# A hybrid decoder layer on one core: token blocks taken one at a time, one block's MLP interleaved with the next block's attention

## The chip, the core and the metric

The kernel runs on one core of a Trainium2 chip. Its time is the device time of one execution in microseconds (us), the median of several runs. TensorE (PE) multiplies matrices into PSUM banks; VectorE (DVE), ScalarE (ACT) and GpSimd (POOL) work element by element; SyncE (SP) issues the DMA transfers. Each engine executes its own queue of instructions strictly in order and waits there for semaphores of the others, so the order in which the program is written decides what can run beside what.

## What is computed

One decoder layer over a prompt of 2,048 tokens and 64 sample tokens (8 sequences of 8), width 1,024. All weights are shared by both groups; there is one layer (DEPTH 1), then a final RMSNorm.

```python
def _mixer_in(x, g_mix, w_in):
    h = _rmsnorm(x, g_mix)
    proj = h @ w_in
    q = proj[..., :ATTN_WIDTH].reshape(B, L, N_KV_HEADS, GROUP, HEAD_DIM)
    ...
    u = proj[..., ATTN_WIDTH + 2 * KV_WIDTH:]
    return q, k, v, u
...
def _layer_tail(x, attn_o, pool_o, mem_k, mem_v, w_out, g_cross, w_cq, w_co, g_ffn, w_up, w_down):
    B, L, _ = x.shape
    x = x + jnp.concatenate([attn_o, pool_o], axis=-1) @ w_out
    h = _rmsnorm(x, g_cross)
    q = (h @ w_cq).reshape(B, L, N_CROSS_HEADS, CROSS_HEAD_DIM)
    s = jnp.einsum('blhd,bmhd->bhlm', q, mem_k).astype(jnp.float32) * (CROSS_HEAD_DIM ** -0.5)
    p = jax.nn.softmax(s, axis=-1)
    o = jnp.einsum('bhlm,bmhd->blhd', p.astype(mem_v.dtype), mem_v).reshape(B, L, D_MODEL)
    x = x + o @ w_co
    h = _rmsnorm(x, g_ffn)
    x = x + jnp.square(jax.nn.relu(h @ w_up)) @ w_down
    return x
...
    for l in range(DEPTH):
        q, k, v, u = _mixer_in(xp, g_mix[l], w_in[l])
        attn_o = _window_attn_prompt(q, k, v, attn_sinks[l])
        ...
        pool_o, pool_new = _pool_mix(u, u_prev, 0, w_pool[l], pool_scale[l])
        mem_k, mem_v = _mem_kv(mem_prompt, g_mem[l], w_ck[l], w_cv[l])
        xp = _layer_tail(xp, attn_o, pool_o, mem_k, mem_v, w_out[l], g_cross[l], w_cq[l], w_co[l],
                         g_ffn[l], w_up[l], w_down[l])
        ...
        q, k, v, u = _mixer_in(xs, g_mix[l], w_in[l])
        attn_o, k_buf, v_buf = _window_attn_sample(q, k, v, cache_win_k[l], cache_win_v[l], attn_sinks[l])
        ...
        xs = _layer_tail(xs, attn_o, pool_o, cache_mem_k[l], cache_mem_v[l], w_out[l], g_cross[l],
                         w_cq[l], w_co[l], g_ffn[l], w_up[l], w_down[l])
```

The attention has a window of 128 tokens, sinks and ALiBi; the pooling mixer subtracts causal means over 2, 4, 8 and 16 tokens. Keys and values of the memory (and the last window's keys, values and pool inputs) are outputs as well. All in fp32.

## The kernel before

**Products.** Every fp32 operand is split in two parts, hi and lo, of a rounded type, and each product is three matmuls: hi·hi, hi·lo, lo·hi (lines 111 to 113 in `mm3`, 280 to 282 in `dense`). Activations are kept with the width on the 128 partitions and tokens in the free dimension, so that a matmul has a 128x128 piece of a weight and as many columns as the block has tokens.

**Weights.** `Stream` holds the list of all weight tiles, 128x1024 each (512 KB), in order of use. `emit` takes one: SyncE loads it to a raw tile `f` (L131), ACT casts it to the hi tile (L132), DVE subtracts to the lo tile (L133); both are named `w` in the views. `next` hands out the oldest, `pump` prepares more while tiles are free. There are 12 `w` tiles (six pairs) and six raw tiles.

**Prologue.** `prologue` computes the memory's keys and values (weights `wck`, `wcv`), folds wcq into the keys (`a_s`, 8 tiles) and wco into the values (`b_s`, 8 tiles), so that cross attention of the prompt needs one product A to the scores and one product B back. The pool projection is folded into w_out (`wo_s`).

**Superblocks.** The tokens are six blocks: 384, 384, 384, 384, 256 and 256 + 64 sample. `SBLOCKS` puts them in three pairs. `superblock` takes a pair through all stages, and each weight pair that is handed out serves both blocks before it is given back (`order` and `seq` in `dense` set which block goes first in which chunk). Stages of a superblock: in-projection (10 weights); window attention (units of one 128-token tile and one of two key heads: QK L668, scores to a tile L669, normalise L690, transposes L699, product with v L716/L717); output projection (8 weights); cross attention (A 8 weights, softmax L929 to L935, transposes L911; B 8 weights); MLP with `up` and `down` alternating in groups of four weights (32 and 32). `mix` alternates attention's steps with the rest of the in-projection; the last superblock also mixes `cross` with `sample_cross`, which loads the samples' own memory (`wcq`, `cmk`, `cmv`, `wco`).

**Norms.** `Norm` squares on ACT (L205), adds on POOL (L206), sums over partitions by a matmul with ones (L214), takes ln and exp (L217 on), and `apply` scales and splits (L232 to L235). A list `later` with `flush` places a norm's second half behind some steps of the other block. The next superblock's first norm is emitted ahead of the last `down` groups.

**MLP.** After `up` a group is evacuated by ACT with relu (L1122), squared on POOL (L1123), cast on ACT (L1125), its lo part formed on DVE (L1126). `down` adds to x on DVE (L1156). A final norm (L1173) and the store of y (L1175) follow.

**PSUM.** Four `mm` banks for products, four `aux` banks for attention, norms and transposes.

Of the kernel before, what the change touches and what calls it, by code (L numbers as in the profile page):

```python
# [36 lines left out]
class Slots:  # L37
# [3 lines left out]

    def get(self):
        return self.free.popleft()
# [8 lines left out]
def kernel(ctx: ExitStack, tc: tile.TileContext, io, nW=12, nF=6, nT=8):  # L52
# [40 lines left out]

    def rnd(ps, hi, lo, scale=None):
        if scale is None:
            nc.scalar.copy(hi, ps)
            nc.vector.tensor_tensor(lo, ps, f32(hi), ALU.subtract)
# [10 lines left out]
    def mm3(ps, ks, Wh, Wl, Hh, Hl, first=True, final=True):  # L108
        last = len(ks) - 1
        for i, k in enumerate(ks):  # L110
            nc.tensor.matmul(ps, Wh(k), Hh(k), start=first and i == 0, stop=False)  # L111
            nc.tensor.matmul(ps, Wh(k), Hl(k), start=False, stop=False)  # L112
            nc.tensor.matmul(ps, Wl(k), Hh(k), start=False, stop=final and i == last)  # L113

    class Stream:
        def __init__(self):
# [3 lines left out]
            self.resF = 0  # L120

        def add(self, key, *raw, eng=None):
            self.items.append((key, raw, eng or nc.vector))

        def emit(self):
            key, raw, eng = self.items.popleft()
            th, tl = WS.get(), WS.get()
            r = FS.get()
# [4 lines left out]
            eng.tensor_tensor(tl[:], r[:, 0:1024], f32(th[:]), ALU.subtract)  # L133
            FS.put(r)
            self.ready.append((key, th, tl))

        def pump(self):
            while self.items and len(WS.free) - 2 >= self.resW and len(self.ready) < 5:
                if len(FS.free) - 1 < self.resF:
                    break  # L140
                self.emit()
# [9 lines left out]
    S = Stream()  # L151
    CIN = (0, 1, 2, 3, 4, 5, 6, 8, 7, 9)
    FINC, N1W, N1Q = 2, 4, 4
    N1C = ("ck", 4)
    LW = (0, 6, 6)
    for n in ("ck", "cv"):
        for c in range(8):
            S.add((n, c), io["w" + n][c])
    for c in range(8):
        S.add(("cq", c), io["wcqt"][c])  # L160
    for c in range(8):
        S.add(("co", c), io["wco"][c])
    for s in range(3):
        for c in CIN:
            S.add(("in", s, c), io["win"][c])
            if s == 0 and c in (0, 1):
                for g in range(2):
                    S.add(("wop", 2 * c + g), io["wop"][2 * c + g])
        for c in range(8):
            S.add(("wo", s, c), io["woa"][c], wo_s[c])  # L170
        for hf in range(2):
            for kp in range(4):
                S.add(("A", s, hf, kp), a_s[hf, kp])
        for c in range(8):
            S.add(("B", s, c), b_s[c])
        for g in range(9):
            for c in range(4):
                if g < 8:
                    S.add(("up", s, g, c), io["wup"][4 * g + c])
            for c in range(4):  # L180
                if g > 0:
                    S.add(("dn", s, g - 1, c), io["wdn"][4 * (g - 1) + c])

    class Norm:
# [5 lines left out]
        def sq(self, k, eng=None):  # L190
            n = self.n
            if self.on_pe:
                t = TS.get()
                if eng is None:
                    nc.scalar.activation(t[:, 0:n], self.x(k), AF.Square)
                else:
                    eng.tensor_tensor(t[:, 0:n], self.x(k), self.x(k), ALU.mult)
                nc.tensor.matmul(self.pm[:, 0:n], ones[:], t[:, 0:n], start=k == 0, stop=k == 7)
# [4 lines left out]
            else:  # L203
                t = TS.get()
                nc.scalar.activation(t[:, 0:n], self.x(k), AF.Square)  # L205
                nc.gpsimd.tensor_tensor(self.acc[:, 0:n], self.acc[:, 0:n], t[:, 0:n], ALU.add)  # L206
                TS.put(t)

        def fin(self):
            n = self.n  # L210
            pm = self.pm
            if not self.on_pe:
                pm = AUX.get()
                nc.tensor.matmul(pm[:, 0:n], ones[:], self.acc[:, 0:n], start=True, stop=True)  # L214
# [11 lines left out]
        def apply(self, g, hi, lo, piece=8):  # L226
            n = self.n
            for k in range(8):
                if k and k % piece == 0:
                    yield  # L230
# [27 lines left out]
    def order(nch, head, tail):  # L258
        out = []
        for lo_, hi_, outer in ((0, head, True), (head, nch - tail, False), (nch - tail, nch, True)):  # L260
            if outer:
                out += [(c, b) for b in (0, 1) for c in range(lo_, hi_)]
            else:
                out += [(c, b) for c in range(lo_, hi_) for b in (0, 1)]
        return out

    def dense(keys, blks, hi, lo, evac, head=2, tail=3, after=None, piece=8, seq=None):
        nch = len(keys)
        loaded, left, done = {}, {}, {0: 0, 1: 0}
        fetched = 0  # L270
        for c, b in seq or order(nch, head, tail):
            while fetched <= c:
# [1057 lines left out]
```

## Time and profile before

| | us |
|---|---|
| median of 3 runs | 2643.78 (2640.39 to 2644.97) |
| span of the profiled execution, first to last instruction | 2639.7 |
| ACT hi casts, 330 | 346.9 |
| DVE lo subtractions, 330 | 422.8 |
| relu, square and split of the MLP on POOL (L1123), 192 | 219.0 |
| additions of `down` on DVE (L1156), 384 | 199.7 |

The profile lists for each engine its busy time, for groups of instructions their number, busy time, mean duration and the idle time before them with the releaser, and for any stretch of time the busy time of each engine in it. `mm<-act,w` means that a tile named mm was written from tiles act and w. The number behind L is the line in the kernel. Matmuls overlap, so their durations (some 0.3 us) are longer than the distance from one start to the next; a stage's rate is better read as a number of matmuls in a stretch. By stretches, the prologue with the first norms takes 0 to about 132 us, then each superblock has a mixed part of some 396 us (in-projection, attention, projection, cross) and an MLP of 330 to 462 us.

### The profile page before, as it was taken

To read this page: it belongs to the slowest core of one execution; us is meant where nothing else is said; L and a number is where in the kernel's file an instruction comes from. 1 tells how busy PE (TensorE), PEld (TensorE's weight loads), DVE (VectorE), ACT (ScalarE), POOL (GpSimd) and SP (SyncE) were. 2 spreads that over 40 slices of the span, in tenths; PEclk is the share of its full clock that TensorE was granted. 3 is DMA by queue.
4 is the path that set the end of the run, shared out by engine and by line. 5 is a ranking of instruction groups with operands and counts; after the bars stand their busy time and mean duration, and the time that the engine had idled before them with its cause. 6 is when DMAs were issued, how large, how long until landed. Compare 5 with 4: busy or idle time off the path is not lost. (4 is left out here: it accounts for less than half of the span.)

```text
span 2639.7 us, 39195 instructions
## 1 busy us (share of the span) xinstructions
PE 2565.7 (97%) x15725; PEld 2458.0 (93%) x15725; DVE 1302.4 (49%) x2276; ACT 984.2 (37%) x1923; POOL 680.7 (26%) x730
## 2 busy tenths in 40 slices
PE   7899999999999999999999999999999999999998
PEld 7798979999999999997999999999999669999998
DVE  7568453633333357936363333334766646334334
ACT  6666342422222244834342222223355434332231
POOL 3215322411111153433241111113334214111111
PEclk9999999999999999999999999999999999999999
DMA  7843212211111123131111111112414473222210
GB/s 261 260 130 101 72 49 74 71 64 63 61 62 64 56 72 113 45 132 56 65 58 63 65 64 64 65 56 71 140 60 149 176 266 112 87 80 81 88 57 37
DMA packets 92251, 244.76 MB, mean 93 GB/s; under 512 B 16740, under 2 KB 31524, under 8 KB 90916
## 3 DMA queue, kind: packets, MB, share of 16 engines
q1 hardware_dynamic: 92068, 242.25, 26.9%
q8 instruction: 123, 2.02, 0.3%
q14 instruction: 60, 0.49, 0.1%
HBM read 219.53 MB, written 22.69 MB: 92 GB/s over the span
## 5 line engine op out<-in xcount | busy, mean ns | idle before, releaser
L281 PE MATMUL mm<-act,w 128*128 128x384 f32 (+2 forms) x2784 | 899.1, 323 | 6.5 <-DVE act L235 5.0
L280 PE MATMUL mm<-act,w 128*128 128x384 f32 (+2 forms) x2784 | 902.8, 324 | 2.5 <-ACT act L623 1.6
L282 PE MATMUL mm<-act,w 128*128 128x384 f32 (+2 forms) x2784 | 897.4, 322 | 1.1 <-DVE w L133 0.9
L132 ACT CAST w<-f 128x1024 fp32r<-128x1024 f32 x330 | 346.9, 1052 | 737.4 <-PE mm L112 453.9
L133 DVE TENSOR_TENSOR w<-f,w 128x1024 fp32r<-128x1024 f32 x330 | 422.8, 1286 | 317.9 <-ACT w L132 312.0
L111 PE MATMUL mm<-act,w 128*128 128x384 f32 (+2 forms) x1728 | 554.1, 321 | 13.6 <-ACT act L372 8.3
L112 PE MATMUL mm<-act,w 128*128 128x384 f32 (+2 forms) x1728 | 550.3, 318 | 0.0
L113 PE MATMUL mm<-act,w 128*128 128x384 f32 (+2 forms) x1728 | 549.8, 318 | 0.0
L281 PEld LDWEIGHTS mm<-act,w 128*128 128x128 f32 x2784 | 527.3, 189 | 16.3 <-DVE act L235 6.7
L280 PEld LDWEIGHTS mm<-act,w 128*128 128x128 f32 x2784 | 527.4, 189 | 7.2 <-issue 2.3
L282 PEld LDWEIGHTS mm<-act,w 128*128 128x128 f32 x2784 | 527.3, 189 | 1.8 <-DVE w L133 1.6
L1123 POOL TENSOR_TENSOR t<-t 128x384 f32<-128x384 f32 (+2 forms) x192 | 219.0, 1141 | 1034.8 <-ACT t L1122 1034.8
L1156 DVE TENSOR_TENSOR x<-mm,x 128x384 f32<-128x384 f32 (+2 forms) x384 | 199.7, 523 | 326.5 <-PE mm L113 326.5
L111 PEld LDWEIGHTS mm<-act,w 128*128 128x128 f32 x1728 | 328.6, 190 | 15.8 <-ACT act L372 8.3
L112 PEld LDWEIGHTS mm<-act,w 128*128 128x128 f32 x1728 | 328.3, 190 | 1.2 <-DVE act L373 0.2
L113 PEld LDWEIGHTS mm<-act,w 128*128 128x128 f32 x1728 | 328.4, 190 | 0.1
L206 POOL TENSOR_TENSOR t<-t,t 128x384 f32<-128x384 f32 (+2 forms) x168 | 203.0, 1209 | 348.9 <-ACT t L205 331.4
L1126 DVE TENSOR_TENSOR act<-t,act 128x384 fp32r<-128x384 f32 (+2 forms) x192 | 103.2, 537 | 300.4 <-ACT act L1125 300.4
L1125 ACT CAST act<-t 128x384 fp32r<-128x384 f32 (+2 forms) x192 | 93.8, 488 | 237.5 <-POOL t L1123 237.5
L1122 ACT ACTIVATE t<-mm 128x384 f32<-128x384 f32 (+2 forms) x192 | 88.2, 459 | 95.2 <-PE mm L282 94.2
L205 ACT ACTIVATE t<-x 128x384 f32<-128x384 f32 (+2 forms) x140 | 68.4, 499 | 145.4 <-DVE x L1085 64.9
L111 PE MATMUL mm<-w,act 128*128 128x512 f32 x288 | 116.7, 406 | 3.2 <-ACT f L330 1.7
(184 smaller groups left out, 2199.0 us busy)
## 6 DMA issues: line engine op xcount, KB each, us to landing
f<-in_wup SPq DMA_DIRECT2D x96, 512.0 KB, 3.5
f<-in_wdn SPq DMA_DIRECT2D x96, 512.0 KB, 3.5
f<-in_win SPq DMA_DIRECT2D x30, 512.0 KB, 3.6
f<-a_s SPq DMA_DIRECT2D x24, 512.0 KB, 3.2
f<-b_s SPq DMA_DIRECT2D x24, 512.0 KB, 4.2
x<-in_x SPq DMA_DIRECT2D x6, 1536.0 KB, 7.1
f<-in_wco SPq DMA_DIRECT2D x16, 512.0 KB, 4.9
f<-in_cmk SPq DMA_DIRECT2D x16, 512.0 KB, 4.5
```

The source lines that it names most:

```text
L111: nc.tensor.matmul(ps, Wh(k), Hh(k), start=first and i == 0, stop=False)
L112: nc.tensor.matmul(ps, Wh(k), Hl(k), start=False, stop=False)
L113: nc.tensor.matmul(ps, Wl(k), Hh(k), start=False, stop=final and i == last)
L132: nc.scalar.copy(th[:], r[:, 0:1024])
L133: eng.tensor_tensor(tl[:], r[:, 0:1024], f32(th[:]), ALU.subtract)
L206: nc.gpsimd.tensor_tensor(self.acc[:, 0:n], self.acc[:, 0:n], t[:, 0:n], ALU.add)
L280: nc.tensor.matmul(ps[:, 0:n], w8(th)[:, k, :], hi(b, k), start=k == 0, stop=False)
L281: nc.tensor.matmul(ps[:, 0:n], w8(th)[:, k, :], lo(b, k), start=False, stop=False)
L282: nc.tensor.matmul(ps[:, 0:n], w8(tl)[:, k, :], hi(b, k), start=False, stop=k == 7)
L1123: nc.gpsimd.tensor_tensor(q[:, 0:n], r[:, 0:n], r[:, 0:n], ALU.mult)
L1126: nc.vector.tensor_tensor(lo, q[:, 0:n], f32(hi), ALU.subtract)
L1156: nc.vector.tensor_tensor(bl.x(m), ps[:, 0:n], bl.x(m), ALU.add)
```

## The change

Blocks are no longer paired. `SBLOCKS` becomes six blocks, each through all stages on its own, and each weight is split anew for each block. Stages are generators: `early` (first norm, in-projection, pool mix, window attention, second load of x), `late_` (output projection, cross norm, the sample's cross attention in the last block, A, B, ffn norm), `mlp`, and `prologue`. They yield between small pieces of work, with a number: how many ns should pass, by an estimate of TensorE's time that `mmul` and `trans` keep in `busy`, before this generator is resumed. `run` interleaves several of them: it resumes the one that is least far along, as a share of the total given with it. At the end of the program these calls stand:

- the prologue with `early` of block 0;
- `late_` of block 0 with `early` of block 1;
- the MLP of block 0 with `late_` of block 1;
- the MLP of block s with `early` and `late_` of block s+1, for s = 1 to 4;
- the MLP of block 5 alone.

There are two weight streams. S1 has the in-, output, A and B weights of blocks 1 to 5 and block 0's in-projection, with six tiles `w0_` (three pairs, of which one holds the keys while attention runs) and four raw tiles `f`, shared with attention, folds and the sample's loads. S2 has the prologue, the rest of block 0 and all MLPs, with six tiles `w1_` and two raw tiles `g`. A and B weights are loaded straight to the lo tile, without a raw one (`ext=False`). PSUM: three `mm` banks for each stream and two `aux`. The prologue's order is now keys, A fold, values, B fold, pool fold, and the memory norm's squares are added on DVE. The cross attention loops over weights outside and tiles inside (`kp` before `c0`), its softmax following for the whole half. The samples' window outputs are copied DRAM to DRAM. The last block's final norm sums its squares on PE.

```diff
-SBLOCKS = [
-    [(0, 384, 0), (384, 384, 0)],
-    [(768, 384, 0), (1152, 384, 0)],
-    [(1536, 256, 0), (1792, 256, 64)],
-]
+SBLOCKS = [[(0, 384, 0)], [(384, 384, 0)], [(768, 384, 0)], [(1152, 384, 0)], [(1536, 256, 0)], [(1792, 256, 64)]]
+NBLK = 6
...
-    ACTS = Slots([sb(f"act{i}", 4 * NB, F32R) for i in range(16)])
-    WS = Slots([sb(f"w{i}", 1024, F32R) for i in range(nW)])
-    FS = Slots([sb(f"f{i}", 1088) for i in range(nF)])
-    TS = Slots([sb(f"t{i}", 400) for i in range(nT)])
-    XT = [sb(f"x{i}", 3136) for i in range(2)]
-    MM = Slots([psp.tile([P, 512], F32, name=f"mm{i}", tag=f"mm{i}") for i in range(4)])
-    AUX = Slots([psp.tile([P, 512], F32, name=f"aux{i}", tag=f"aux{i}") for i in range(4)])
+    ACTT = [sb(f"act{i}", 4 * NB, F32R) for i in range(16)]
+    ACTS = Slots(ACTT)
+    WS = [Slots([sb(f"w{q}_{i}", 1024, F32R) for i in range(6)]) for q in range(2)]
+    FS = [Slots([sb(f"f{i}", 1088) for i in range(4)]), Slots([sb(f"g{i}", 1024) for i in range(2)])]
+    F0 = FS[0]
+    TS = Slots([sb(f"t{i}", 400) for i in range(6)])
+    TM = Slots([sb(f"tm{i}", 384) for i in range(3)])
+    XT = [sb(f"x{i}", 3072) for i in range(2)]
+    MM = [Slots([psp.tile([P, 512], F32, name=f"mm{q}{i}", tag=f"mm{q}{i}") for i in range(3)]) for q in range(2)]
+    AUX = Slots([psp.tile([P, 512], F32, name=f"aux{i}", tag=f"aux{i}") for i in range(2)])
...
+        def __init__(self, q):
+            self.W, self.F, self.M = WS[q], FS[q], MM[q]
...
+            key, raw, ext = self.items.popleft()
+            th, tl = self.W.get(), self.W.get()
+            r = self.F.get() if ext else f32(tl[:])
...
+            nc.vector.tensor_tensor(tl[:], r[:, 0:1024], f32(th[:]), ALU.subtract)
+            if ext:
+                self.F.put(r)
...
+    S1, S2 = Stream(0), Stream(1)
     CIN = (0, 1, 2, 3, 4, 5, 6, 8, 7, 9)
...
+    for s in range(NBLK):
+        for c in CIN:
+            S1.add(("in", s, c), io["win"][c])
+        if s > 0:
+            late_keys(S1, s)
...
+    late_keys(S2, 0)
...
+    def dense(S, keys, n, hi, lo, evac):
+        for c, key in enumerate(keys):
+            th, tl = S.next(key)
+            ps = S.M.get()
+            for k in range(8):
+                mmul(ps[:, 0:n], w8(th)[:, k, :], hi(k), start=k == 0, stop=False)
+                mmul(ps[:, 0:n], w8(th)[:, k, :], lo(k), start=False, stop=False)
+                mmul(ps[:, 0:n], w8(tl)[:, k, :], hi(k), start=False, stop=k == 7)
+                if k < 7 and k % 2 == 1:
+                    yield 0
+            S.put(th, tl)
+            evac(c, ps)
+            S.M.put(ps)
+            yield 0
...
+    def run(*gens):
+        ops = [[g, tot, 0.0, 0.0] for g, tot in gens]
+        now = 0.0
+        while ops:
+            ok = [o for o in ops if o[3] <= now] or [min(ops, key=lambda o: o[3])]
+            o = min(ok, key=lambda o: o[2] / o[1])
+            b0 = busy[0]
+            w = next(o[0], -1)
+            d = busy[0] - b0
+            o[2] += d
+            now += d
+            if w == -1:
+                ops.remove(o)
...
+                now = max(now, o[3]) if len(ops) == 1 else now
+                o[3] = now + w
...
+    blk = [make_blk(s) for s in range(NBLK)]
+    run((prologue(), 105e3), (early(blk[0]), 50e3))
+    run((late_(blk[0], S2), 120e3), (early(blk[1]), 60e3))
+    for s in range(NBLK):
+        gens = [(mlp(blk[s]), 266e3)]
+        if s == 0:
+            gens.append((late_(blk[1], S1), 125e3))
+        elif s + 1 < NBLK:
+            def both(bl):
+                yield from early(bl)
+                yield from late_(bl, S1)
+            gens.append((both(blk[s + 1]), 190e3))
+        run(*gens)
```

The three places below are rows of the engines' queues, in order; `x4` behind a row stands for four of them in a row.

TensorE in the attention of a later block, before the change: `mm_109` is a product of the in-projection of the same superblock (L280 to L282), `aux` of L668 are scores of attention, w_79 and w_80 the keys.

```order
L634 MATMUL aux_113<-ident,f_94 128x128
L668 MATMUL aux_114<-w_79,act_69 128x256
L668 MATMUL aux_114<-w_80,act_69 128x256
L668 MATMUL aux_111<-w_79,act_69 128x256
L668 MATMUL aux_111<-w_80,act_69 128x256
L280 MATMUL mm_109<-act_76,w_83 128x384
L281 MATMUL mm_109<-act_78,w_83 128x384
```

TensorE in the attention of a later block after the change; `mm_111` and `mm_112` are banks of S2, here an MLP, w_0_79 the keys, L105 the matmul of every form and L109 every transpose.

```order
L109 MATMUL aux_115<-ident,x_106 128x128
L105 MATMUL aux_114<-w_0_79,act_69 128x256 x2
L105 MATMUL mm_111<-act_64,w_1_86 128x384
L105 MATMUL mm_111<-act_68,w_1_86 128x384
L105 MATMUL mm_111<-act_64,w_3_88 128x384
L105 MATMUL mm_111<-act_64,w_1_86 128x384
L105 MATMUL mm_111<-act_68,w_1_86 128x384
L105 MATMUL aux_115<-w_0_79,act_69 128x256 x2
L105 MATMUL mm_111<-act_64,w_3_88 128x384
L105 MATMUL mm_112<-act_63,w_4_89 128x384
L105 MATMUL aux_114<-w_0_79,act_69 128x256 x2
```

The products between attention's rows now belong to another block's MLP instead of the in-projection of the same superblock.

TensorE in the attention of block 0, before: `mm_107` is the in-projection of the second block.

```order
L668 MATMUL aux_111<-w_89,act_67 128x128
L668 MATMUL aux_111<-w_90,act_67 128x128
L668 MATMUL aux_112<-w_89,act_67 128x128
L668 MATMUL aux_112<-w_90,act_67 128x128
L280 MATMUL mm_107<-act_63,w_88 128x384
L281 MATMUL mm_107<-act_65,w_88 128x384
L282 MATMUL mm_107<-act_63,w_86 128x384
```

The same place after the change; the rows of `mm_109` are attention's product with v.

```order
L109 MATMUL aux_115<-ident,x_106 128x128
L105 MATMUL aux_114<-w_0_79,act_75 128x256 x2
L109 MATMUL aux_114<-ident,x_106 128x128 x4
L105 MATMUL aux_115<-w_0_79,act_75 128x256 x2
L105 MATMUL mm_109<-act_63,vt 128x512
L105 MATMUL aux_115<-w_0_79,act_75 128x256 x2
L105 MATMUL aux_114<-w_1_80,act_76 128x256 x2
```

Between attention's rows no other product stands any more.

SyncE's queue among the MLP's weight loads, before: raw tiles f_91 to f_96 in turn.

```order
L131 DMA f_96<-in_wup 128x1024
L131 DMA f_91<-in_wdn 128x1024
L131 DMA f_92<-in_wdn 128x1024
L131 DMA f_93<-in_wdn 128x1024
L131 DMA f_94<-in_wdn 128x1024
L131 DMA f_95<-in_wup 128x1024
```

The same queue after the change, at the end of one MLP and the beginning of the next: g_95 and g_96 are the two raw tiles of S2, x_106 the tile of x of both.

```order
L151 DMA g_96<-in_wup 128x1024
L151 DMA g_95<-in_wup 128x1024
L1144 DMA out_y<-x_106 128x768 x4
L151 DMA g_96<-in_wup 128x1024
L151 DMA g_95<-in_wup 128x1024
L447 DMA x_106<-in_x 128x3072
L151 DMA g_96<-in_wup 128x1024
```

Two raw tiles take turns where six did, and the stores of y and a block's load of x stand among the weight loads.

More of the change, by code (lines that the diff above doesn't have):

```diff
@@ L458, in norm1 @@
         for k in range(8):
             nm.sq(k)
[L461 to L476 removed]
+            if k % 2:
+                yield 1500
@@ L514, in in_evac @@
                     nc.vector.tensor_tensor(kz[kv][1][o, d], src, f32(kz[kv][0][r, d]), ALU.subtract)
-                    if b == 1 and not last:
+                    if not last:
                         for hl in range(2):
@@ new lines, in early, with units @@
+        bl.h1.free()
+        S.resF = 2
+        while late:
+            yield 2000
+            tick()
+        def units():
+            for c0 in range(0, bl.np, P):
+                tl = Tile_()
+                tl.bl, tl.c0 = bl, c0
+                tl.k0 = P if bl.t0 + c0 == 0 else 0
+                for kv in range(2):
+                    u = Tile_()
+                    u.t, u.kv = tl, kv
+                    yield u
+        us_ = list(units())
+        if smp:
+            yield from attn_sample()
```

907 lines of the change are left out of this document (394 added, 513 removed).

## The prediction

> **What bounds the kernel now.** I read the clock line and the table of stages first.
>
> ```profile
> core 0: 2639.7 us, clock 0.992
> PE 2565.7 (97%) x15725; PEld 2458.0 (93%) x15725; DVE 1302.4 (49%) x2276; ACT 984.2 (37%) x1923; POOL 680.7 (26%) x730
> core 0: us, PE busy (x) PEld busy (x) DVE busy (x) ACT busy (x) POOL busy (x), PEclk, DMA share, GB/s
> 0.00:132.00 132.00, 108.98 (x723) 101.09 (x724) 87.31 (x117) 84.48 (x145) 42.28 (x39) 0.96 0.78 261
> 132.00:528.00 396.00, 385.20 (x2130) 359.31 (x2129) 225.18 (x442) 183.92 (x405) 130.74 (x153) 1.00 0.25 83
> 528.00:990.00 462.00, 462.00 (x2663) 461.47 (x2663) 174.58 (x246) 122.79 (x193) 87.69 (x77) 1.00 0.19 63
> 990.00:1386.00 396.00, 387.16 (x2150) 361.71 (x2150) 247.90 (x477) 183.50 (x406) 143.58 (x158) 1.00 0.23 78
> 1386.00:1848.00 462.00, 462.00 (x2667) 461.95 (x2666) 165.52 (x238) 121.03 (x193) 81.06 (x76) 1.00 0.19 64
> 1848.00:2244.00 396.00, 375.35 (x2537) 329.23 (x2536) 245.05 (x499) 181.03 (x398) 131.80 (x165) 0.97 0.43 150
> 2244.00:2574.00 330.00, 330.00 (x2476) 330.00 (x2476) 129.33 (x203) 96.16 (x162) 55.95 (x55) 1.00 0.23 78
> 2574.00:2639.70 65.70, 55.06 (x392) 53.25 (x390) 27.54 (x58) 11.33 (x24) 7.62 (x8) 0.96 0.10 37
> ```
>
> TensorE (PE) is the bound: 97% busy, while VectorE (DVE) has 49% and ScalarE (ACT) 37%. But busy hides gaps between pipelined matmuls, so I count instead. From 528 to 990 us, an MLP stretch, 2663 matmuls of 384 columns take 462 us: 0.1735 us each, with nothing idle. Three rows of the timeline fix the 512-column period.
>
> ```profile
> 1200.79 0.39 PE L111 MATMUL mm<-w,act 128*128 128x512 f32 x1
> 1201.02 0.39 PE L112 MATMUL mm<-w,act 128*128 128x512 f32 x1
> 1201.24 0.39 PE L113 MATMUL mm<-w,act 128*128 128x512 f32 x1
> ```
>
> They start 0.227 apart; a line through the two sizes gives 0.119 for 256 columns and 0.146 for 320. Count times period, form by form, is the work of a stage; the rest is **loss**. For the first 132 us:
>
> ```profile
> L111 PE MATMUL mm<-act,w 128*128 128x256 f32 x192 | 58.1, 303 | 13.6 <-ACT act L372 8.3 <-DVE t L380 4.5 <-ACT f L330 0.8
> L111 PE MATMUL mm<-w,act 128*128 128x512 f32 x32 | 12.8, 404 | 3.0 <-ACT f L330 1.7 <-ACT w L132 1.3
> L282 PE MATMUL mm<-act,w 128*128 128x384 f32 x14 | 4.7, 335 | 0.0
> ```
>
> Each row is one of three product lines with like counts: 576×0.119 + 96×0.227 + 42×0.1735, with some 2 us of small ones, is about 100 us, so 32 are lost. The same count gives a loss of 22 in 132–528 (attention and cross of the first two blocks), 1 in 528–990, 20 in 990–1386, 1 in 1386–1848, 50 in 1848–2244 (some 20 to 2046, 30 behind it: the sample's cross attention, B and the last ffn norm), 2 in 2244–2574 and 12 at the end. That is **140 of 2639.7 us**, and 2,500 of work. The matmuls are the same after the change, so the whole question is what becomes of the 140.
>
> **What the change costs.** Each weight split serves one block, not two: 36 prologue splits stay, 3×98 become 6×98. So 330 become 624, 294 more.
>
> ```profile
> L132 ACT CAST w<-f 128x1024 fp32r<-128x1024 f32 x330 | 346.9, 1052 | 737.4 <-PE mm L112 453.9
> L133 DVE TENSOR_TENSOR w<-f,w 128x1024 fp32r<-128x1024 f32 x330 | 422.8, 1286 | 317.9 <-ACT w L132 312.0
> ```
>
> 294×1.052 is 309 us more on ACT (984 to 1293, 49%), 294×1.286 is 378 more on DVE (1302 to 1680, 64% of the span). On SyncE's queue 294×0.5 MB are added: 242 MB become about 390, 27% of the DMA time become 43%. All of this lies beside PE, and none is in the sum as such; what hides it is that in the MLP a weight holds PE for 24 matmuls, 24×0.1735 = 4.16 us, while its split takes DVE 1.29. Without that cover the 378 us would stand in the time.
>
> A split is also a DVE instruction that reads two SBUF tiles while GpSimd (POOL) squares beside it:
>
> ```profile
> 601.96 0.83 POOL L1123 TENSOR_TENSOR t<-t 128x384 f32<-128x384 f32 x1 [1.96 <-ACT t L1122]
> ...
> 606.41 1.23 DVE L133 TENSOR_TENSOR w<-f,w 128x1024 fp32r<-128x1024 f32 x1 [2.48 <-ACT w L132]
> 606.84 1.48 POOL L1123 TENSOR_TENSOR t<-t 128x384 f32<-128x384 f32 x1 [4.05 <-ACT t L1122]
> 607.66 0.33 SPq L131 DMA_DIRECT2D f<-in_wdn  x1
> ```
>
> The square alone takes 0.83, beside a split 1.48. If each of the 294 new splits holds POOL so for 0.65, that is 191 us on an engine with 680 of 2639: POOL goes to 33%. I take no loss on PE, with 0 to 30 as bounds, since a group's square may be late by one group of 4.16 us: the stream has three PSUM banks. The Trainium skill, "SBUF — State Buffer", section "Who interferes with whom", says that a DVE instruction with two SBUF inputs contends with a GpSimd one that reads SBUF, under an exclusive lock where the later one waits to the end. These rows agree (1.48 against 0.83); by that rule DVE could be the one that waits, which would put part of the 191 on DVE and its share to 71% at most.
>
> **What it moves.** (1) *The start.* Block 0's in-projection is set between the prologue's matmuls, so waits on evacuations are filled. The first wait, 8.3 on the first weight's activations, has no other work, nor have the matmuls before the first x is normalised. I take 22 for 32; ends 17 and 35 (all small waits gone; two more streams of loads on a queue at 78%).
>
> (2) *Attention of block 0* has no partner: in the new order its QK rows, transposes and PV rows stand alone. DVE work there, by kind:
>
> ```profile
> L669 DVE CUSTOM_DVE_ANT_0 x<-aux,cst,vec 128x256 f32<-128x256 f32 x120 | 54.7, 479 | 11.0 <-PE aux L668 8.2 <-POOL x L690 0.8 <-POOL t L604 0.7
> L97 DVE TENSOR_TENSOR w<-aux,w 128x512 fp32r<-128x512 f32 x44 | 29.1, 673 | 0.8 <-ACT w L96 0.8
> L721 DVE TENSOR_TENSOR cp<-mm,cp 64x512 f32<-64x512 f32 x32 | 22.0, 686 | 1.4 <-ACT cp L720 0.6
> L97 DVE TENSOR_TENSOR act<-cp,act 128x512 fp32r<-128x512 f32 x16 | 11.5, 721 | 0.0
> L690 DVE TENSOR_SCALAR x<-x,st 128x256 f32<-128x256 f32 x30 | 11.2, 374 | 0.1
> ```
>
> Together 128.9 us for the 32 units (16 tiles, two head groups): 4.0 each. PE needs per unit 8×0.119 + 8×0.11 + 4×0.227 = 2.7. Six units are 24 of DVE, with 6 splits (7.7) and small ones (some 4) 36; PE has 16 and some 3 beside. Loss 17 (bounds 8, the six splits elsewhere, and 25, when the stages wait for each other as well). Block 1's attention has a partner, 47 us of PE against 47.5 of DVE. How such a stretch goes stands in the trace:
>
> ```profile
> 1056.00:1122.00 66.00, 64.47 (x401) 59.57 (x400) 62.45 (x182) 54.63 (x153) 29.49 (x45) 1.00 0.14 45
> 924.00:990.00 66.00, 66.00 (x379) 65.47 (x378) 37.35 (x55) 27.46 (x51) 33.61 (x31) 1.00 0.23 72
> ```
>
> With DVE at 62.45 of 66 (attention beside in-projection) 4.5 us are lost by count; with 37.35 (a norm beside MLP) under 1. I take 5 for block 1.
>
> (3) *Norms.* One whose chain nothing covers shows in the chain of waits:
>
> ```profile
> 2202.89 0.99 DVE t L219
> ...
> 2205.03 2.29 DVE t L232 x4
> 2207.32 1.74 DVE act L235 x2
> ...
> 2210.37 1.57 POOL act L235 x2
> ...
> 2215.75 0.21 PE mm L280
> 2215.96 0.21 PE mm L281
> ```
>
> From the statistics to the first matmul it is some 9 us of which PE fills little, and the matmuls behind it go at 0.21 for a 256-column one, not 0.119: a clock at half for a while. The Trainium skill, "TensorE: Matmul & The Clock Gate", "Part 1: The HAM clock gate", gives half rate after an idle window of about 3.4 us; the mean clock of 0.992 agrees in kind, and by it closing all gaps could save some 14 us more, an estimate from that page, not in the sum. Before, two blocks covered each other's norms in most places. After, block 0's ffn norm stands alone ahead of the first MLP: 9, and two more norms of blocks 0 and 1 cost 1 each. With attention 1 that is 16 between block 0's attention and its MLP (bounds 8 and 30).
>
> (4) *Blocks 1 to 5* run their attention and cross stages beside an MLP, whose 768 to 640 matmul groups are always ready. DVE per stage, by the count of (2) with the splits of both streams, is 44 us for 52 of PE in blocks 2 and 3, 27 for 36 in block 4 and 30 for 33.5 in block 5: shares of 75 to 90%, between the two rows above (57 and 95%, losses under 1 and 4.5). I take 4 for a block, 20 for five. What stands against it: all engines run in order, so an evacuation of the MLP queued on DVE behind an attention instruction that waits for PE holds PE. Bounds 5 and 74 (rival 1).
>
> (5) *The sample's tail.* The sample cross attention follows block 5's attention; by the order MLP 4 is over before it ends, so the same gaps as behind 2046 stay: 26 for 30 (8 for late loads, 10 for the norm before the last MLP, 8 else). Bounds 15 and 40.
>
> (6) *MLP alone.* About 60, 45, 45 and 114 us of MLPs 0 to 3, and MLP 5. Its loads have two raw tiles in turn, where six were. A turn:
>
> ```profile
> f<-in_wup SPq DMA_DIRECT2D x96, 512.0 KB, 3.5
> f<-in_wcv SPq DMA_DIRECT2D x8, 512.0 KB, 5.4
> ```
>
> 3.5 to land, 0.33 to issue (the row above, just behind the split), 1.05 and 1.29 to split: 6.2 for two tiles, 3.1 a weight, against 4.16 of PE with 384 columns and 24×0.146 = 3.5 with 320. It holds, narrowly, for the last block; at 5.4 to land (when the queue is full, as in the prologue) it is 8.1, 4.05 a weight. A and B loads go straight to a weight tile, and wait on SyncE for PE to release it; MLP loads queue behind, covered by two pairs ready (8.3 us); so do they behind the second load of a block's x, which waits for the last reader of attention, since attention works in the same tile. I take 4 in all (bounds 1 and 26, rival 2). The end stays: 13 for 12.
>
> **The sum.** 22 + 17 + 16 + 20 + 26 + 4 + 13 = 118 lost for 140: −22. The profiled run becomes 2639.7 − 22 = 2617.7; the median of the runs stands 4.1 above its span (2643.8), so about **2622 us**, −0.8%. From the bounds that decide, not all at once, this case has 2595 to 2638.
>
> **The rivals.** (R1, slower) *In-order VectorE.* In 990–1386 DVE was busy 247.9 of 396, 63%, and 20 us were lost, 5%. Afterwards DVE has 64% over the whole, so about 1,470 us of mixed stages may lose 5%: 74 instead of 20, +54, 2676 (2650 to 2710). The mechanism is a PE that waits for an evacuation or a split which stands on DVE behind an instruction that itself waits; from 42 us of it, 2.9% of the mixed stretches, the saving of 22 is used up and the kernel is slower. For it: the like share of DVE and the like stages lose 5% now. Against: the quoted loss is in stretches with a DVE share of 95%, and the mixed MLP groups have three banks of their own. Chance 0.25. (R2) *Two raw tiles.* If landing takes 4.7 or more, 7.4 a turn, MLP 5 gets 3.7 to 3.9 a weight for 3.5: 64×0.35 = 22, and some in the prologue: 2650. Chance 0.10. (R3) *Nothing gained.* The uncovered front part (attention, ffn norm) gives back all that mixing saves: about 2640. Chance 0.10. (R4) *Full cover.* Start 17, attention 0 and what follows 25, the mixed stages 5, tail 15, MLP alone 1, end 13: 76 lost for 140, −64, 2580. Chance 0.10. The forecast has 0.45.
>
> **Range.** It reaches to R4 and to the middle of R1: 2580 to 2690, with 0.2 left out. Some 0.2% (5 us) is what a measurement of this kernel can tell. Faster: forecast and R4, 0.55. Same: R3, 0.10. Slower: R1 and R2, 0.35.
>
> **What would show it.** Right: counts per stretch that lose about 17 to 25 us around block 0's attention and under 1.5% where an MLP is mixed; DVE 1,680 us; MLP 5 at 0.146 a matmul. Wrong: PE waiting for L132's or L133's successors in MLP stretches (R2), PE's waits for VectorE evacuations spread over all mixed stretches (R1), or a clock under 0.99. It would fall altogether if PE's matmul count or its full-rate period differed.

## The result and the profile after

The changed kernel takes 2806.74 us (median of 4 runs, 2802.93 to 2811.01), the kernel before 2642.27 (4 runs, 2640.39 to 2644.97): a ratio of 1.0617, 95% interval 1.06 to 1.0633. It is **6.2% slower**, 164 us; forecast was 22 faster.

The clock and the busy shares of the changed kernel, and stretches of it cut at the seams between blocks (columns as before the change):

```profile
core 0: 2806.9 us, clock 0.972
PE 2633.2 (94%) x15725; PEld 2492.4 (89%) x15725; DVE 1633.5 (58%) x2577; ACT 1267.4 (45%) x2217; POOL 750.3 (27%) x771
0.00:132.00 132.00, 113.62 (x773) 110.38 (x774) 82.66 (x115) 73.11 (x117) 23.34 (x31) 0.96 0.71 241
132.00:264.00 132.00, 108.26 (x482) 88.45 (x481) 78.31 (x159) 74.15 (x162) 44.95 (x60) 0.87 0.52 164
264.00:462.00 198.00, 181.11 (x974) 165.21 (x973) 126.14 (x232) 102.36 (x210) 64.33 (x72) 0.98 0.31 106
462.00:726.00 264.00, 264.00 (x1482) 257.19 (x1481) 135.47 (x180) 103.40 (x159) 55.36 (x49) 1.00 0.37 126
726.00:990.00 264.00, 244.72 (x1370) 237.26 (x1370) 164.88 (x277) 124.49 (x231) 86.89 (x88) 0.96 0.35 122
1188.00:1452.00 264.00, 243.89 (x1369) 235.60 (x1368) 165.28 (x275) 124.64 (x232) 89.25 (x90) 0.97 0.35 122
2112.00:2376.00 264.00, 242.38 (x1738) 232.81 (x1737) 174.60 (x314) 134.23 (x260) 88.18 (x99) 0.95 0.49 162
2376.00:2574.00 198.00, 175.66 (x1201) 135.60 (x1200) 98.37 (x169) 76.50 (x124) 37.41 (x42) 0.94 0.61 209
```

The matmuls are the same, 15,725, and their full rate too. Counted with the median distance of each form from one start to the next (the sample's small scores, which start in pairs, by the pair), the work is some 2,512 us. The rest of the span is the loss: 128 us before and 295 after. It is small between the seams: 462 to 726, an MLP with block 1's cross part beside it, loses 1 us. It is large at the front and at each seam, where an MLP ends and the next one starts with the first norm and attention of the following block: there the rows show idle TensorE and a clock under 1.

| stretch | loss forecast | loss after |
|---|---|---|
| start, 0 to 132 | 22 | 29 |
| block 0 up to its MLP, 132 to 462 | 17 + 16 | 74 |
| blocks 1 to 5 beside MLPs, MLPs alone, 462 to 2376 | 20 + 4 | 138 |
| sample's end, 2376 to 2574 | 26 | 39 |
| last MLP and end | 13 | 15 |
| sum | 118 | 295 |

TensorE's waits in the whole of the changed kernel: what waited, for what, us in total, times, the longest.

```profile
PE aux L105 <- POOL t L235: 35.0, 12, 7.1
PE mm L105 <- ACT w L152: 19.9, 5, 8.4
PE aux L105 <- DVE vt L114: 14.4, 6, 4.1
PE mm L105 <- DVE x L1120: 11.2, 5, 3.7
PE mm L105 <- DVE w L153: 10.5, 13, 1.8
PE aux L105 <- DVE st L664: 9.2, 7, 4.5
...
PE aux L105 <- DMA f<-in_cmv: 8.7, 5, 3.6
```

The first row is the matmul with ones that sums a norm's squares. The timeline of the first seam shows why it waits:

```profile
801.78 4.08 SPq L1144 DMA_DIRECT2D out_y<-x  x4
808.77 0.33 SPq L447 DMA_DIRECT2D x<-in_x  x1
817.90 0.53 ACT L232 ACTIVATE t<-x 128x384 f32<-128x384 f32 x1 [0.39 <-DMA x<-in_x]
818.92 8.31 POOL L235 TENSOR_TENSOR t<-t,t 128x384 f32<-128x384 f32 x7 [1.95 <-ACT t L234]
827.29 1.65 PE L105 MATMUL aux<-t,ones 128*128 128x384 f32 x2 [7.13 <-POOL t L235]
828.16 6.03 PE L105 MATMUL mm<-act,w 128*128 128x384 f32 x24
```

Block 2's x goes to the tile that block 0's y has just left, so its load is issued at 808.8 and the first square starts at 817.9; seven additions on POOL follow; and the matmul with ones stands in TensorE's queue ahead of MLP matmuls that could run. It costs 7.1 us, and the 24 matmuls behind it take 6.03 where 4.16 is their full rate. The stretches show why, with the clock granted to TensorE behind the counts of POOL:

```profile
827.00:831.00 4.00, 3.71 (x10) 3.11 (x11) 1.01 (x2) 2.03 (x4) 1.01 (x2) 0.50 0.02 8
831.00:834.00 3.00, 3.00 (x18) 3.00 (x17) 2.80 (x4) 1.22 (x3) 1.57 (x1) 0.97 0.10 15
```

For 4 us the granted clock is 0.50 and only 10 matmuls start; then 18 start in 3 us. From the first matmul to the last, waits over 0.6 us make up some 169 of the 295 (before: 57), and matmuls at about half rate (1.7 to 2.1 times their distance) some 62 (before: 28).

A little later the first scores of block 2 wait for v:

```profile
911.44 0.84 POOL L583 TENSOR_TENSOR t<-x 128x398 f32<-128x398 f32 x1
911.52 1.84 DVE L153 TENSOR_TENSOR w<-g,w 128x1024 fp32r<-128x1024 f32 x1
912.36 3.70 POOL L583 TENSOR_TENSOR t<-t 128x396 f32<-128x396 f32 x3
...
916.09 1.16 DVE L596 SCALAR_TENSOR_TENSOR t<-t,x 128x384 f32<-128x384 f32 x1 [2.73 <-POOL t L583]
...
918.36 0.28 DVE L114 TENSOR_TENSOR vt<-aux,vt 128x128 fp32r<-128x128 f32 x1
...
918.70 0.80 PE L105 MATMUL aux<-w,act 128*128 128x256 f32 x2 [4.11 <-DVE vt L114]
```

The split of v takes 0.28 us, but stands on VectorE behind a weight's split and a pool-mix instruction that itself waits for GpSimd.

### The profile page after: what moved, and what is told of

Its sections match the earlier page's. It is cut to its first block, busy times and chain, and to the rows that moved or that the text cites. A ratio compares the mean times of both kernels' runs of the same rounds, so it can differ in the third digit from the quotient of the medians.

```text
span 2806.9 us, 40920 instructions
## 1 busy us (share of the span) xinstructions
PE 2633.2 (94%) x15725; PEld 2492.4 (89%) x15725; DVE 1633.5 (58%) x2577; ACT 1267.4 (45%) x2217; POOL 750.3 (27%) x771
## 5 line engine op out<-in xcount | busy, mean ns | idle before, releaser
L105 PE MATMUL mm<-act,w 128*128 128x384 f32 (+2 forms) x13088 | 2233.5, 325 | 57.3 <-ACT w L152 14.1
L105 PEld LDWEIGHTS mm<-act,w 128*128 128x128 f32 x13088 | 2126.0, 191 | 100.1 <-ACT w L152 16.4
L153 DVE TENSOR_TENSOR w<-g,w 128x1024 fp32r<-128x1024 f32 x428 | 539.5, 1261 | 286.1 <-ACT w L152 283.3
L152 ACT CAST w<-g 128x1024 fp32r<-128x1024 f32 x428 | 448.5, 1049 | 464.5 <-PE mm L105 387.3
L1103 POOL TENSOR_TENSOR tm<-tm 128x384 f32<-128x384 f32 (+2 forms) x192 | 246.4, 1284 | 697.1 <-ACT tm L1102 695.2
L1120 DVE TENSOR_TENSOR x<-mm,x 128x384 f32<-128x384 f32 (+2 forms) x384 | 198.5, 519 | 197.7 <-PE mm L105 197.3
L105 PE MATMUL mm<-w,act 128*128 128x512 f32 x864 | 216.2, 399 | 8.0 <-ACT w L152 5.8
L105 PEld LDWEIGHTS mm<-w,act 128*128 128x128 f32 x864 | 162.9, 191 | 44.0 <-ACT w L152 7.3
L153 DVE TENSOR_TENSOR w<-w,w 128x1024 fp32r<-128x1024 f32 x96 | 118.9, 1240 | 123.5 <-ACT w L152 122.9
L153 DVE TENSOR_TENSOR w<-f,w 128x1024 fp32r<-128x1024 f32 x100 | 124.0, 1240 | 66.5 <-ACT w L152 64.8
L152 ACT CAST w<-f 128x1024 fp32r<-128x1024 f32 x100 | 105.0, 1050 | 112.5 <-PE mm L105 81.7
L105 PE MATMUL mm<-ar,w 128*128 128x320 f32 (+1 forms) x448 | 111.0, 305 | 0.8 <-DVE x L1120 0.4
L1102 ACT ACTIVATE tm<-mm 128x384 f32<-128x384 f32 (+2 forms) x192 | 87.6, 457 | 18.4 <-PE mm L105 15.0
L105 PE MATMUL aux<-w,act 128*128 128x256 f32 (+1 forms) x256 | 61.6, 333 | 26.6 <-DVE vt L114 14.4
```

Source lines behind the costliest of these rows:

```text
L105: return nc.tensor.matmul(o, w, x, **kw)
L152: nc.scalar.copy(th[:], r[:, 0:1024])
L153: nc.vector.tensor_tensor(tl[:], r[:, 0:1024], f32(th[:]), ALU.subtract)
L1102: nc.scalar.activation(r[:, 0:n], ps[:, 0:n], AF.Relu)
L1103: nc.gpsimd.tensor_tensor(q[:, 0:n], r[:, 0:n], r[:, 0:n], ALU.mult)
L1120: nc.vector.tensor_tensor(bl.x(m), ps[:, 0:n], bl.x(m), ALU.add)
```

## The experiments

Most are single runs, compared with single runs of the kernel before beside them (2637.7 to 2646.1); the changed kernel's own four runs differ by 8 us, and differences under some 8 us in a time say nothing. Where a loss is given by "us of work", the stretch is cut by TensorE's progress through its work, so that stages stay in line; the 8.3 us ahead of the first matmul are then left out.

**Do the additional splits cost?** In the kernel before, each split twice:

```diff
-            nc.scalar.copy(th[:], r[:, 0:1024])
-            eng.tensor_tensor(tl[:], r[:, 0:1024], f32(th[:]), ALU.subtract)
+            for _ in range(2):
+                nc.scalar.copy(th[:], r[:, 0:1024])
+            for _ in range(2):
+                eng.tensor_tensor(tl[:], r[:, 0:1024], f32(th[:]), ALU.subtract)
```

> The kernel before, with each weight's ACT cast and DVE subtraction done twice from the same raw tile (330 more of each, where the change adds 294; loads and order as before). Theory A (the splits themselves cost: DVE and ACT are fuller, POOL and PE wait for them): at least 60 us more than before, 2700 or above, spread over all stages. Theory B (splits hide behind TensorE; the loss of the change is where waiting instructions stand in the queues at the seams between blocks): under 15 us more, below 2660, MLP stretches still at 0.1735 us a matmul.

2758.9, 117 us more. Its page line and three of its stretches:

```profile
PE 2610.1 (95%) x15725; PEld 2477.3 (90%) x15725; DVE 1672.9 (61%) x2606; ACT 1300.3 (47%) x2253; POOL 661.3 (24%) x730
594.00:990.00 396.00, 396.00 (x2287) 396.00 (x2286) 187.13 (x239) 143.12 (x191) 42.67 (x48) 1.00 0.19 62
990.00:1452.00 462.00, 438.41 (x2398) 407.68 (x2397) 323.48 (x562) 240.96 (x482) 171.75 (x181) 0.99 0.22 74
1914.00:2376.00 462.00, 426.07 (x2761) 372.33 (x2760) 317.00 (x580) 239.00 (x474) 148.23 (x182) 0.95 0.42 137
```

VectorE and ScalarE are about as busy as after the change. An MLP stretch still has 2287 matmuls in 396 us, 0.1732 each: there a second split is free. All 117 us stand in the prologue and the mixed parts: 34 in the prologue, whose splits the change does not add to, and about 30, 24 and 31 in the three mixed parts, which hold 102 of the 330 splits. Neither theory was right as put: splits cost, but only among instructions that TensorE is waiting for.

In the changed kernel, the MLP's weights subtracted on 64 of 1024 columns, then cast so too, then all weights from block 0's MLP on:

```diff
+            m = 64 if key[0] in ("up", "dn") else 1024
-            nc.vector.tensor_tensor(tl[:], r[:, 0:1024], f32(th[:]), ALU.subtract)
+            nc.vector.tensor_tensor(tl[:, 0:m], r[:, 0:m], f32(th[:, 0:m]), ALU.subtract)
```

> The changed kernel, with the subtraction for the MLP's weights done on 64 of 1024 columns only, so that the lo parts of the MLP weights are left out but for these: DVE loses some 384 x 1.1 = 420 us and has less to do than before the change. Theory A: most of the 165 us comes back, 2700 or below. Theory B: the seams stay as they are, 2780 to 2810.

> The changed kernel with cast and subtraction of the MLP's weights on 64 of 1024 columns only (the weights' other columns are left out: what the tiles held stands there). With the narrow subtraction alone it was 2755. If ACT's casts cost at the seams as DVE's subtractions do (relu and norm pieces stand behind them): 2715 to 2740. If only DVE matters: 2748 to 2760. What is left above 2644 is then no matter of split work.

> The changed kernel with cast and subtraction on 64 of 1024 columns for every weight from block 0's MLP on (in-, output-, A and B weights of blocks 1 to 5 too; the other columns of these weights are left out). With the MLP's alone it was 2750. Theory A2 (split work that stands in ACT's and DVE's queues among norm and attention pieces is most of the loss; doubling 138 such splits in the kernel before cost 117 us): 2680 to 2715. Rival B3 (the places are it: block 0 alone at the front, the sample at the end, norm statistics ahead of MLP products): 2730 or above.

2755.1, 2750.4 and 2723.4. VectorE's 384 subtractions were worth 52 us, ScalarE's casts 5 more, which single runs can't tell from nothing, and the other weights 27: 83 of the 164. By us of work, 61 of it came at the seams (435 to 2050), 15 around the sample's end (2050 to 2300) and 9 at the front. In the last, VectorE was busy for 1140 us, less than before the change (1302), and yet it took 86 us more than the kernel before. So narrow splits give **half** of the loss back. That is not quite the price of the added splits: the last run narrows 554 of the 624, and the change added 294.

> The changed kernel with the in-, output-, A and B weights of block 1 stored as hi and lo in DRAM and loaded so for blocks 2 to 5: 136 splits fewer (DVE 174 us, ACT 143 us), 136 more loads of 0.5 MB and 68 stores. All is computed. Theory A2: each split that leaves a mixed stretch gives 0.2 to 0.4 us, 2755 to 2780. Rival: loads land later at 45% DMA time and take the gain back, within 10 us of 2807.

> As the one before, with block 0's up weights kept in the same way for blocks 1 to 3 (96 splits fewer again), the first norm later (25 for 6, 19 us by itself) and the two totals raised (4 us by itself). If the parts add: 2700 to 2745. If they share one loss: 2750 to 2775. Above it the loads are late.

> The kernel before with the in-, output-, A and B weights of the first superblock stored as hi and lo and loaded so for the other two: 68 splits fewer, 68 more loads and 68 stores. All is computed. Theory A2, from the other side (such splits cost where stages mix, also in the kernel before): 990 to 1386 us loses 20 now, 1848 to 2244 some 50; a fourth of it goes, 2620 to 2635. Rival (before the change these splits are covered): within 5 us of 2644, or above by the stores in 132 to 528.

2806.5, 2778.9 and 2643.0 (2637.7 beside it). Parts that were stored once and loaded again gave nothing in the first run, in the second some 4 us beyond what its two other edits give by themselves, which single runs can't tell from nothing; in the second, TensorE's waits have a new row, 18.6 us:

```profile
PE mm L106 <- DMA w<-keep: 18.6, 20, 3.3
```

In the kernel before, 68 fewer splits save nothing in sum, while 330 more cost 117: the two later mixed parts lose 3 us less each, and the first, where the stores stand, loses 9 more. There splits are nearly covered, and the cover has an end.

**Do waiting instructions stand in the wrong place?** The first norm later, then the additions of all norms on VectorE as well:

```diff
-            yield 6000
+            yield 25000
         nm = Norm(n, bl.x)
...
-                (eng or nc.gpsimd).tensor_tensor(self.acc[:, 0:n], self.acc[:, 0:n], t[:, 0:n], ALU.add)
+                (eng or nc.vector).tensor_tensor(self.acc[:, 0:n], self.acc[:, 0:n], t[:, 0:n], ALU.add)
```

> The changed kernel, with the estimated time between a block's load of x and its first squares 25 instead of 6 us (one number). Theory B1 (at each of the four seams the matmul with ones of the next block's norm stands in TensorE's queue ahead of MLP matmuls while x is still on its way, since its tile must first be stored as y; 7 us each and a halved clock behind it): the waits on L235 at four seams go, 28 us, with clock 30 to 40, so 2765 to 2780. Rival B2 (the seam's loss is DVE and POOL queues being full, whatever the place): the wait moves along with the matmul, within 10 us of 2807.

> The changed kernel with the first norm later (25 for 6, which by itself gave 2788) and all norms' additions of squares on VectorE instead of GpSimd (0.56 us each instead of 1.2). If the norms' chain on GpSimd is what the statistics wait for: 2765 to 2780. If VectorE's queue is what the seams lack: 2788 to 2810.

2787.7 and 2769.8: 19 and 18 us. At the first seam the 7.1 us wait is gone; less came than forecast for the first, since some of the wait moved to the MLP's relu and to v. That VectorE, the fuller engine, took on the additions and the time fell speaks for the chain of the norm, not for VectorE's share.

> The changed kernel with 6 in place of 2 us of estimated time ahead of the last pool-mix pieces and 4 us behind them, so that more MLP products stand ahead of the first scores. Theory B1 (first scores wait for v's split, which stands on DVE behind a pool-mix instruction that waits for POOL): the waits on L114 at the seams, 5.6, 5.6 and 2.2 us, go with half a clock's time behind them: 2785 to 2795. Rival B2 (the same DVE and POOL work ends no sooner): within 6 us of 2807.

```diff
         while late:
-            yield 2000
+            yield 6000
             tick()
+        yield 4000
```

2807.9, nothing: at the first seam the wait for v (5.6 us) has gone, and 2.3 us on a score and 3.0 on a transposed tile's split stand in its place, each behind other VectorE work. The rival was right here.

> Split work narrow for all weights from block 0's MLP on (as in the run that gave 2723; these columns are left out), the first norm later (25 for 6) and the two totals raised. If split work and late norms are two causes: the four seams lose some 6 us less each, the front 8 less, 2685 to 2700. If the norm's wait only came of full queues: within 10 us of 2723.

> The run with narrow splits and late norms that gave 2693 (weights' columns left out as there), with the norms' additions on VectorE as well. If the chain on GpSimd is left over at the front and the end too: 2675 to 2685. If GpSimd was only slow because of the splits beside it (its squares took 0.81 us there, 1.28 in the changed kernel): 2689 to 2700.

2693.2 and 2686.4. Split work and late norms are two causes that add: 30 us beyond the narrow splits, though the two raised totals (4 us by themselves) are in it; the additions gave 7 more, within the scatter of single runs, where they gave 18 beside full splits. Between 435 and 2050 us of TensorE's work, the seams, the loss falls from 130 us in the changed kernel to 70 with narrow splits, 39 with late norms too, 32 with the additions moved. The kernel before loses 51 in the same stretch of its work, so the seams are explained by these two. What is left over the kernel before, 44 us, is not there but at the front: up to 352 us of work, where block 0's MLP starts in the new order, the last run loses 89 and the kernel before 41 (there with two blocks beside each other), and behind it the two lose alike (75 and 79).

**The front and the sample's end.**

```diff
-    run((prologue(), 105e3), (early(blk[0]), 50e3))
+    run((prologue(), 105e3))
+    run((early(blk[0]), 50e3))
```

> The changed kernel with the prologue run to its end before block 0's first part begins, instead of mixed with it. If mixing the prologue pays as forecast (10 us at the start): 2815 to 2845. If it costs (block 0's attention stands bare in both, and the loads of two streams share the queue): 2790 to 2807.

2828.5, 22 us more than with mixing. Its first stretch against the row above:

```profile
0.00:132.00 132.00, 105.25 (x676) 91.54 (x676) 68.97 (x100) 70.25 (x116) 15.64 (x19) 0.97 0.81 253
```

676 matmuls for 773: in the new order, mixing the prologue pays.

> The changed kernel with two totals of the interleaving raised (block 0's first part 50 to 90, block 5's 190 to 300), so that block 0's attention stands beside prologue products and block 5's sample part mostly ahead of the end of the MLP before. Theory C1 (those two places lose because TensorE has no other work in its queue there): the 46 us lost around block 0's attention fall to 20 to 30 and the 54 around the sample's end to 25 to 35, so 2755 to 2785. Rival C2 (DVE or the loads bound these stages, with or without products between): within 15 us of 2807.

2802.5, 4 us less, within the scatter, where 20 to 50 were expected. Around block 0's attention (130 to 220 us of work) the loss fell from 41 to 31, at the sample's end (2050 to 2300) from 46 to 43, and in the stretch ahead of that (1850 to 2050) it rose from 31 to 39. Neither theory: products between helped a little, and the rest moved.

> The changed kernel with the first norm later, the totals raised (block 1's first part to 100 too) and 1.8 in place of 0.6 us of estimated time between attention's steps. All is computed. If attention's steps stand too close together (waits on scores, v and transposes, 28 us in the trace, and the clock behind them): 2750 to 2775. If they only move: 2780 to 2800.

2781.2; in it block 1's first attention tile is spoiled, since block 0's softmax writes the same work tile between that tile's two halves, so y is not the layer's there. Instructions and sizes are the same.

> The changed kernel with all repairs of order together that compute everything: first norm later (25 for 6), the two totals raised, norms' additions on VectorE, 1.8 for 0.6 us between attention's steps. Singly they gave 2788 (norm), 2770 with the additions, and 4 us for the totals. If order is half of the loss and split work the other half, order alone gets to 2735 to 2765 and not below 2720; below 2660 the split work would not matter.

2778.2, 8 above the best of its parts, late norms with additions on VectorE. Against that run it loses 10 us less around block 0's attention, but 10 more between 435 and 1700 us of work, 6 more at the start and 3 more at the sample's end. Why attention that is spread out costs there was not taken apart.

**PSUM and mixing.**

> The changed kernel with PSUM shared out as 3 banks for S1, 2 for S2 and 3 aux (changed: 3, 3, 2; before: 4 mm and 4 aux). Theory D1 (two aux banks make attention a chain: scores, DVE, next scores; norms and transposes wait for the same two): waits of aux matmuls on DVE's L664 and L114, 34 us in the changed kernel's trace, fall by half, 2785 or below. Rival D2 (the banks are enough, DVE's queue is the limit): within 8 us of 2807, and above it if two banks are too few for the MLP.

2826.6, 20 us more: two banks are too few for S2 (the waits for L1120 and L1102 rise from 16 to 32 us), and the waits for scores did not fall (9 to 16).

> The changed kernel with each block's attention and cross stages behind the MLP of the block before instead of between its products (the first two interleaved calls as they are). If mixing covers what it is meant to: blocks 2 to 5 show their norms (three of 9 us), attention on DVE (4.0 a unit against 2.7) and softmax bare, 40 to 60 us a block more than the seams' 32, so 2950 or above. If the seams' loss comes from mixing itself (waiting instructions ahead of MLP work): less than 60 us above 2807.

3092.8, 286 us more: mixing does cover; without it each block loses far more than its seam does.

## Why the prediction was wrong

**The step that failed** is (4), "I take 4 for a block, 20 for five". The stretches with blocks 1 to 5 lost 138, MLPs alone included, for 24: 114 of the 177 us by which the sum of losses was short. Another 41 are in (2) and (3), 74 for 33. The step read cover from VectorE's share in two rows (57 and 95%). In the seam from 726 to 990 its share is 62%, near the harmless one of the two, and 31 us are lost. A share says how much an engine has to do, not what stands ahead of the one instruction that TensorE waits for. With narrow splits and late norms, both of which leave TensorE's products alone, the loss there (435 to 2050 us of work) fell from 130 to 39, under the 51 of the kernel before: the missing part of the sum was splits and norms. That the norms cost by their place in the queue is shown by moving them. By which way the splits cost is shown in single places only, such as v's split above: a narrow split also frees its raw tile sooner and holds GpSimd for less time, and no run keeps these apart.

**The cost of the splits.** "None is in the sum as such" was right for MLP stretches (the doubled splits were free there) and wrong wherever attention, norms and cross stages stand: 83 us, most of it at the seams. 64% was forecast as VectorE's share, 58% came. GpSimd was forecast to be held for 191 us more; its busy time rose by 70.

**Norms.** Step (3) counted one uncovered norm, ahead of the first MLP. It missed that a block's x has to wait for the y of the block two before it: one late norm at each of four seams, a wait of 5 to 7 us and the slow clock behind it. Moved later they gave 19 us, with the additions on VectorE 37.

**Attention of block 0**: no product stood beside it, as foretold, but 74 us are lost up to block 0's MLP for 33. The bound was VectorE's work alone; in 132 to 264 it is busy 78 of 132 us. The stages wait for each other, which was only the upper end of a bound. Putting products between them gave some 10 us there. The front (up to 352 us of work) lost 95 us, and 89 with narrow splits and late norms, their additions on VectorE, against 41 in the kernel before; the splits of block 0 were never taken away there, so how much of the rest is theirs stays open.

**The start** came within its bounds, 29 for 22: 3 us were saved of the 10 taken. The first 130 us of work lose 54 in the new order without mixing, 29 with it and 25 in the kernel before: mixing wins back most of what the new order costs there.

**The sample's end** lost 39 for 26. Its starting point was off as well: by the count used here, 1848 to 2244 lost 38 before the change and not 50, 17 of them behind 2046 and not 30, and the 140 of the whole kernel are 128. Late loads were named (8 us); the trace has 8.7 on cmv. Narrow splits gave 15 us around it; the rest is the chain of small steps, and was not taken apart.

**Rivals.** R1 had part of the mechanism, that of the splits and of v: TensorE waits for something that stands on VectorE behind an instruction that itself waits. The late norm, TensorE's largest wait, is not in it. Its price, 5% of the mixed stretches from a stage of the kernel before, was too small: there one split served two blocks, and one block's products covered the other's norm. A seam loses 12% (31 of 264). R2 is refuted by the last MLP, with two raw tiles and nothing beside it:

```profile
2640.00:2706.00 66.00, 66.00 (x452) 66.00 (x451) 35.43 (x46) 27.68 (x41) 14.97 (x11) 1.00 0.44 148
```

452 matmuls of 320 columns in 66 us, 0.146 each.

## What to carry to other kernels

Cover is not a share: before work is moved beside other work, list what will stand in each in-order queue ahead of the instruction that the busiest engine waits for, with what each of these waits for in turn. A matmul that depends on a late load stops everything behind it on TensorE; it belongs so far back that its data are there, and a tile that is reused sets that time. To price work "hidden" by an engine's idle time, double it in the old kernel and see in which stretches it costs.

## What the runs showed of the hardware

GpSimd's squares and VectorE's splits hold each other up. The square of the MLP's activations, in the changed kernel and with all narrow splits:

```profile
L1103 POOL TENSOR_TENSOR tm<-tm 128x384 f32<-128x384 f32 (+2 forms) x192 | 246.4, 1284 | 697.1 <-ACT tm L1102 695.2 <-issue 1.8
```

```profile
L1104 POOL TENSOR_TENSOR tm<-tm 128x384 f32<-128x384 f32 (+2 forms) x192 | 155.8, 811 | 736.8 <-ACT w L153 433.4 <-ACT tm L1103 300.9 <-issue 2.3
```

The same 192 instructions take 1.28 us each beside full subtractions and 0.81 beside narrow ones. In the changed kernel 96 of the 128 squares of 384 columns start while a split runs; their median is 1.42 us, and they end 0.69 behind the split, while a square with no split beside it takes 0.83. It goes the other way as well: with narrow splits, 95 of them start while a square runs and take 0.78 (median) instead of 0.23, to 0.08 behind the square's end. The Trainium skill, "SBUF — State Buffer", section "Who interferes with whom", has the later of two such instructions wait to the other's end; the trace agrees with that in both directions. So VectorE pays too: the weight's split ahead of v above takes 1.84 for 1.23, beside a pool-mix instruction of GpSimd that started 0.08 earlier. Part of what the narrow splits gave may have come through GpSimd, since norms' additions run there; the runs do not tell it apart.
